# A two-layer mixer block in split fp32: the FFN and short-conv products take the high weights times both halves of x in one 512-column matmul

## The chip, the cores and the metric

The kernel runs on one core of one Trainium2 chip. The metric is the device time of one execution in microseconds (us), the median of the runs shown. "TensorE", "VectorE" and "ScalarE" are the core's engines; SBUF is its working memory, PSUM (eight banks of 512 fp32 columns on 128 partitions) is where TensorE writes.

## The reference

256 tokens of width 1024 go through two layers of one kind and a third of another. A layer is FFN, mixer, FFN, each with a norm before and after it; the mixer is a short convolution in the first layer and a gated delta rule in the second. Then come a second mixer (sparse attention and RWKV side by side) and an FFN with a convolution. All of it is fp32.

```python
def swiglu(x, w_gate_up, w_down):
    gate, up = jnp.split(x @ w_gate_up, 2, axis=-1)      # 1024 -> 2 x 2816
    return (jax.nn.silu(gate) * up) @ w_down              # 2816 -> 1024

def short_conv_mixer(x, w_in, conv_w, w_out):
    b, c, v = jnp.split(x @ w_in, 3, axis=-1)             # 1024 -> 3 x 1024
    y = b * causal_depthwise_conv(c * v, conv_w)
    return y @ w_out                                      # 1024 -> 1024

for i in range(DEPTH):                                    # two layers
    ff = swiglu(rms_norm(h, g[0]), ffn_w_gate_up[i, 0], ffn_w_down[i, 0])
    h = h + 0.5 * rms_norm(ff, g[1])
    m_in = rms_norm(h, g[2])
    mix = short_conv_mixer(m_in, ...) if i % 2 == 0 else gated_deltanet_mixer(m_in, ...)
    h = h + rms_norm(mix, g[3])
    ff = swiglu(rms_norm(h, g[4]), ffn_w_gate_up[i, 1], ffn_w_down[i, 1])
    h = h + 0.5 * rms_norm(ff, g[5])
# then the second mixer with its output projection, and an FFN whose hidden width is
# 2 x 2816, convolved over three tokens, gated and projected down to 1024
```

## The kernel before, in words

Activations lie transposed: 128 features on the partitions, 256 tokens along the row. A product is a list of 128 x 128 weight tiles (`Product`, L47): column tiles (128 output features each) times row tiles (128 input features). The first column tiles are taken as a group, row tile by row tile; `groups` names the sizes, and the rest go one by one. There are 968 chunks of four weight tiles, 3872 tiles in all, in the order of `SEQUENCE` (L111).

Every product runs in three matmuls per weight tile, in fp32r (a form of fp32 that TensorE streams in one pass). Weights and operand are each split in a high part and the low rest, and the product is wh xh + wh xl + wl xh (`mm3`, L790). Each matmul has its own load of 128 x 128 weights (the row PEld), also where two in a row use the same weights. Row tiles 0 and 1 of a group of six use another order (`mm3s`, L797).

The weights come by DMA from the SP queue into six raw buffers (`Streamer`, L620); for each chunk ScalarE copies the high half (`whi<-wraw`) and VectorE subtracts for the low one (`wlo<-wraw,whi`), into a ring of seven chunks.

The operand x is h times a gain, split the same way by `split_x` (L815) in `prepare` (L821), without the factor 1/rms of the norm, which is not known yet. `stat_now` (L959) makes 1/rms (`rb`) after the first group with a product with a matrix of ones, in plain fp32, and the evacuation multiplies by it. In the delta rule's input product, the second mixer's `rw` product and the convolution FFN (`cup`), all grouped 6, 2, 2, x is split again with 1/rms in it (`again`, `resplit`, L1050) for the column tiles after these ten.

What is evacuated: an up product's pair of column tiles (gate, up) gets two VectorE products with `rb`, SiLU on ScalarE, a product, a high copy and a low subtract (`swiglu`, L987). Short conv's triples (L1012) and the convolution FFN's pairs (L2108) go through a few VectorE steps per tap. A down product's column goes through `post` (L965): a square, its sum, and the product with its gain. PSUM: with the banks taken in turn, column tiles that are taken one by one share a bank by twos where the evacuation takes pairs or triples; in a group, and in the down products, each has a bank (`dense_steps`, L903).

The order on each engine is written by a planner (`Pace`, L260). It prices each instruction (a matmul: columns / 2400 us + 2.5 ns), builds the graph of what waits for what, tries some list schedules (`ranks`, L335; `schedule`, L363), and `arrange` (L446) fixes the best order. The delta rule and the second mixer weave their own small products between those of the weight stream.

Of the kernel before, what the change touches and what calls it, by code (L numbers as in the profile page):

```python
# [12 lines left out]
F32R = mybir.dt.float32r  # L13
# [61 lines left out]
# The rule's input projection by column tile: queries 0-7, keys 8-15, values 16-31, output gates 32-47, and 48 for beta  # L75
# and the decay. The keys come first, whose inverse takes longest.
# [3 lines left out]
def products():  # L80
    g = {}
    for l in range(2):
        for j in range(2):
            g["up", l, j] = Product("ffn_w_gate_up", (l, j), KD, _blocks(_pairs(0, FF, NF)), [6])
            g["down", l, j] = Product("ffn_w_down", (l, j), NF, _blocks(range(0, D, P)))
# [3 lines left out]
    g["sc_in"] = Product("sc_w_in", (0,), KD, _blocks(c), [6])  # L89
# [148 lines left out]
class Staged:  # L238
    """Work on a sequence of items, whose later stages are issued with the next items' earlier ones."""
# [20 lines left out]
class Pace:  # L260
    """An account, by rough prices in us, of when each engine gets to what is issued to it and when each part of a
    tile was last written and read. Independent sequences of steps are interleaved by it."""
# [17 lines left out]
    def parts(self, ap):  # L280
        """The pieces of its tile that an access pattern touches."""
# [18 lines left out]
    def when(self, *aps):  # L300
        """When everything issued to these is done."""
# [144 lines left out]
    def arrange(self, tc, rank):  # L446
        """Has each engine take what was issued to it in the order of these ranks."""
# [8 lines left out]
    def node(self, engine, op, out, ins, outs, price):  # L456
        """An instruction of the graph, with those that come before it."""
# [132 lines left out]
class Chain:  # L590
    """A sequence of steps with the banks and buffers that it takes in turn."""
# [15 lines left out]
def alternate(*steps):  # L607
    """The sequences in turn, each waiting while another goes on."""
# [11 lines left out]
class Streamer:  # L620
    """Brings the weight tiles on chip ahead of their use, as high and low halves."""
# [43 lines left out]
    def split_to(self, c):  # L665
        """Every chunk before this one."""
# [3 lines left out]
    def split_ahead(self, c):  # L670
        """While chunk c is in use and as long as the engines that split have little else to do."""
# [22 lines left out]
class Kernel:  # L694
    def __init__(self, nc, pool, psum, wstream, params, consts, xt, lowrank, w1, out):
# [9 lines left out]
        self.xh = pool.tile([P, KD, T], F32R, name="xh")  # L705
        self.xl = pool.tile([P, KD, T], F32R, name="xl")
# [14 lines left out]
        self.x0 = [pool.tile([P, T], F32R, name=f"x0{i}") for i in range(2)]  # L721
# [21 lines left out]
    def warm(self):  # L743
        """Products of nothing in use, by which the tensor engine's clock is up when the first operands are there."""
# [8 lines left out]
    def region(self, tag, dtype=F32):  # L753
        """A region of SBUF for a phase's tiles: a new tile in the place of the last one."""
# [3 lines left out]
    def hidden(self, **kept):  # L758
        """Room for both parts of a branch's hidden tiles."""
        a = [kept.get(t) or self.region(t, F32R) for t in ("a0", "a1", "a2")]  # L760
        slot = lambda n: a[n // 16][:, n % 16 * T:(n % 16 + 1) * T]
        self.hid = [(slot(k), slot(NF + k)) for k in range(NF)]
# [16 lines left out]
    def bank(self, n=7):  # L779
        """The next of the first n banks, or of a list of banks."""  # L780
# [9 lines left out]
    def mm3(self, out, xh, xl, start, stop):  # L790
        wh, wl = self.W.next()
        nc = self.nc
        nc.tensor.matmul(out, wh, xh, start=start, stop=False)
        nc.tensor.matmul(out, wh, xl, start=False, stop=False)
        nc.tensor.matmul(out, wl, xh, start=False, stop=stop)

    def mm3s(self, outs, xs, start):  # L797
        """A row tile of a group, the products with the operand's low part last; the first tile's operand may be a sum."""
        mm = self.nc.tensor.matmul
        ws = [self.W.next() for _ in outs]  # L800
        for n, (xh, xl) in enumerate(xs):
# [13 lines left out]
    def split_x(self, k, gain):  # L815
        """The product of h tile k with a gain, split for the tensor engine."""
# [4 lines left out]
    def prepare(self, k, gain, post=None):  # L821
        """h tile k takes its update, and its product with the next gain is split for the tensor engine. Of the first
        tile only the update's is split, which is added to that of h before it."""
        nc = self.nc
        h = self.h[:, k, :]
        if post is not None:
            t = self.temp()
            if k == 0:
                self.first = gain
                nc.pace.hurry = URGENT  # L830
                nc.vector.tensor_mul(self.x0[0], self.fg0, post)
                nc.pace.hurry = 0.0
                nc.vector.tensor_mul(t, self.fg0, post)
                nc.vector.tensor_sub(self.x0[1], t, self.x0[0])
# [16 lines left out]
    def halves(self, out, w, x, **kw):  # L851
        """A product with few columns, on each half of the tensor engine's."""
# [4 lines left out]
    def take(self, *aps):  # L857
        """The next bank of the running sequence, once it and these are ready."""
# [44 lines left out]
    def dense_steps(self, key, x, evac, step, prepare=None, hooks=(), each=None, at_group=None, late=None, banks=7, lead=LEAD, gate=None):  # L903
        """One product: evac gets the PSUM regions of `step` consecutive column tiles; hooks[g] runs when the
# [1313 lines left out]
```

## Time and profile before

| | |
|---|---|
| three runs | 1584.44, 1581.71, 1584.09 us; median 1584.09 us |
| the profiled execution | span 1586.4 us, first to last instruction (the page gives no other time of its own) |
| TensorE matmul / weight load rows busy | 99% / 96%, 13544 each |
| VectorE / ScalarE busy | 76% / 65% |
| DMA | 261 MB, 165 GB/s in the mean |

The profile shows one execution. Where instructions of one engine overlap, busy time counts the overlap once, while the mean of one is its full length; the pace of an engine is read from starts, or from a stretch's length over its count. Matmul ends are modelled. All operations carry one line (L576, the helper that issues them), so groups are told apart by their tiles: `xh`, `xl` and `x` are the operand's halves and the first tile's (x0), `a` the hidden tiles, `whi` and `wlo` the split weights.

Where the stages lie, in us from the start: up(0,0) to 130, down(0,0) to 194, short conv in 194 to 264 and out to 288, up(0,1) to 415, down(0,1) to 478, up(1,0) to 601, down(1,0) to 665, delta rule to 930, up(1,1) to 1058, down(1,1) to 1121, second mixer to 1374 with its output product to about 1396, convolution FFN up to 1520 and down to the end.

### The profile page before, as it was taken

To read this page: it belongs to the slowest core of one execution; us is meant where nothing else is said; L and a number is where in the kernel's file an instruction comes from. 1 tells how busy PE (TensorE), PEld (TensorE's weight loads), DVE (VectorE), ACT (ScalarE), POOL (GpSimd) and SP (SyncE) were. 2 spreads that over 40 slices of the span, in tenths; PEclk is the share of its full clock that TensorE was granted. 3 is DMA by queue.
4 is the path that set the end of the run, shared out by engine and by line. 5 is a ranking of instruction groups with operands and counts; after the bars stand their busy time and mean duration, and the time that the engine had idled before them with its cause. 6 is when DMAs were issued, how large, how long until landed. Compare 5 with 4: busy or idle time off the path is not lost.

```text
span 1586.4 us, 35927 instructions
## 1 busy us (share of the span) xinstructions
PE 1569.7 (99%) x13544; PEld 1517.6 (96%) x13544; DVE 1202.2 (76%) x2527; ACT 1026.9 (65%) x2153; POOL 10.4 (1%) x24
## 2 busy tenths in 40 slices
PE   9999999999999999999999999999999999999999
PEld 9999999999999999989898999999987877999999
DVE  7776597877658777689996778765887955889973
ACT  7555566765557557578887866555782766578763
POOL 0000000000000000000000000000010000000000
PEclk9999999999999999999999999999998989999999
DMA  8666556566665667525342456666533312566664
GB/s 275 192 186 187 180 176 186 170 190 187 184 185 167 201 193 245 180 79 168 116 138 81 135 159 201 187 187 184 168 106 101 120 35 87 172 187 188 187 194 118
DMA packets 142670, 261.14 MB, mean 165 GB/s; under 512 B 15904, under 2 KB 17952, under 8 KB 142368
## 3 DMA queue, kind: packets, MB, share of 16 engines
q1 hardware_dynamic: 142496, 258.84, 53.9%
q8 instruction: 106, 1.74, 0.4%
q14 instruction: 68, 0.56, 0.1%
HBM read 257.73 MB, written 1.05 MB: 163 GB/s over the span
## 4 chain that ended last, share of the span: by engine, by line
PE 93%; DVE 3%; ACT 2%; issue 1%; DMA 0%; SPq 0%; DVEq 0%
PE bank L576 93%; DVE a L576 1%; ACT a L576 1%; DVE wlo L576 1%; ACT stm L576 1%; DMA wraw<-wstream 0%; DVE arG L576 0%; ACT whi L576 0%; DVE stm L576 0%; ACT arG L576 0%; DVE fg L576 0%; DVE xl L576 0%; DVE tmp L576 0%; DVE acc L576 0%; ACT pad L576 0%
## 5 line engine op out<-in xcount | busy, mean ns | idle before, releaser
L576 ACT ACTIVATE whi<-wraw 128x512 fp32r<-128x512 f32 x956 | 599.3, 630 | 440.9 <-PE bank L576 335.5
L576 DVE TENSOR_TENSOR wlo<-wraw,whi 128x512 fp32r<-128x512 f32 x956 | 653.0, 688 | 291.2 <-ACT whi L576 282.6
L576 PE MATMUL bank<-xh,whi 128*128 128x256 f32 x2688 | 753.1, 284 | 6.1 <-DVE stm L576 3.6
L576 PE MATMUL bank<-xh,wlo 128*128 128x256 f32 x2688 | 751.6, 284 | 0.0
L576 PE MATMUL bank<-xl,whi 128*128 128x256 f32 x2688 | 745.7, 282 | 0.7 <-DVE xl L576 0.7
L576 PEld LDWEIGHTS bank<-xh,whi 128*128 128x128 f32 x2688 | 507.6, 190 | 15.2 <-issue 6.0
L576 PEld LDWEIGHTS bank<-xl,whi 128*128 128x128 f32 x2688 | 504.1, 189 | 8.8 <-issue 6.6
L576 PEld LDWEIGHTS bank<-xh,wlo 128*128 128x128 f32 x2688 | 502.0, 189 | 6.9 <-issue 6.0
L576 PE MATMUL bank<-a,whi 128*128 128x256 f32 x2272 | 411.0, 283 | 0.2
L576 PEld LDWEIGHTS bank<-a,whi 128*128 128x128 f32 x2272 | 353.6, 191 | 1.2 <-DVE a L576 0.4
L576 PE MATMUL bank<-a,wlo 128*128 128x256 f32 x1136 | 321.6, 283 | 0.0
L576 PEld LDWEIGHTS bank<-a,wlo 128*128 128x128 f32 x1136 | 217.2, 191 | 0.0
L576 DVE TENSOR_TENSOR tmp<-bank,rb 128x256 f32<-128x256 f32 x176 | 66.3, 418 | 8.0 <-ACT rb L576 0.6
L576 PE MATMUL bank<-a 64*128 64x256 f32 (+3 forms) x192 | 41.4, 397 | 1.4 <-DVE arG L576 1.4
L576 ACT ACTIVATE xh<-h,par 128x256 fp32r<-128x256 f32 x70 | 34.0, 498 | 12.0 <-DVE h L576 9.9
L576 ACT ACTIVATE arG<-bank 128x256 f32<-128x256 f32 (+2 forms) x87 | 37.8, 443 | 5.2 <-PE bank L576 4.9
L576 DVE SCALAR_TENSOR_TENSOR arG<-arG,par 128x256 f32<-128x256 f32 x88 | 40.0, 477 | 0.0
L576 ACT ACTIVATE a<-tmp 128x256 fp32r<-128x256 f32 x88 | 35.7, 406 | 6.5 <-DVE tmp L576 6.3
L576 DVE TENSOR_TENSOR acc<-acc,tmp 128x256 f32<-128x256 f32 x92 | 38.4, 418 | 2.0 <-ACT acc L576 0.9
L576 DVE TENSOR_TENSOR a<-tmp,a 128x256 fp32r<-128x256 f32 x88 | 36.7, 417 | 3.8 <-ACT a L576 3.8
L576 ACT ACTIVATE tmp<-tmp 128x256 f32<-128x256 f32 x88 | 35.4, 407 | 3.8 <-DVE tmp L576 3.7
L576 DVE TENSOR_TENSOR tmp<-tmp,tmp 128x256 f32<-128x256 f32 x88 | 36.7, 417 | 0.0
(253 smaller groups left out, 1229.5 us busy)
## 6 DMA issues: line engine op xcount, KB each, us to landing
wraw<-wstream SPq DMA_DIRECT2D x968, 256.0 KB, 2.8
arG<-cmp_w SPq DMA_DIRECT2D x1, 1024.0 KB, 4.7
out_dram<-h SPq DMA_DIRECT2D x8, 128.0 KB, 2.7
con<-consts SPq DMA_DIRECT2D x1, 734.0 KB, 4.7
h<-xt SPq DMA_DIRECT2D x1, 512.0 KB, 6.5
a<-lowrank SPq DMA_DIRECT2D x1, 512.0 KB, 4.0
par<-params SPq DMA_DIRECT2D x1, 283.5 KB, 4.8
h<-xt SPq DMA_DIRECT2D x2, 128.0 KB, 3.4
```

Of the source, the lines that this page charges most:

```text
L576: i = f(*args, **kw)
```

## The change

x, the first tile's update x0 and the hidden tiles put each tile's high and low half side by side, so that the two are 512 columns in one row. A column tile for which `wide` holds takes a whole bank: one matmul of the high weights with both halves, 512 columns, and one of the low weights with the high half into the bank's first 256. The two halves of the bank are added when it is evacuated, by a ScalarE copy and a VectorE add. Wide are: in the four up products and cup the column tiles after the first 10 (of 44), in sc_in after the first 9 (of 24), and all but the last of the eight in the down products, sc_out, out2 and cdown. The up products take groups of 6, 2, 2, sc_in of 6, 3, and x is split again with 1/rms in it before the wide tiles of these five; their evacuation no longer multiplies by `rb`. The gate and up tiles move from the general buffers to eight slots in the region arG. Descriptions in the code are removed as well, which changes nothing.

```diff
-            g["up", l, j] = Product("ffn_w_gate_up", (l, j), KD, _blocks(_pairs(0, FF, NF)), [6])
+            g["up", l, j] = Product("ffn_w_gate_up", (l, j), KD, _blocks(_pairs(0, FF, NF)), [6, 2, 2])
...
-    g["sc_in"] = Product("sc_w_in", (0,), KD, _blocks(c), [6])
+    g["sc_in"] = Product("sc_w_in", (0,), KD, _blocks(c), [6, 3])
...
+        self.x = pool.tile([P, KD, 2, T], F32R, name="x")
+        self.xh, self.xl = self.x[:, :, 0], self.x[:, :, 1]
...
+        self.hid = [a[k // 8][:, k % 8 * 2 * T:(k % 8 + 1) * 2 * T].rearrange("p (w t) -> p w t", w=2) for k in range(NF)]
...
+    def mm2(self, out, x, start, stop):
+        wh, wl = self.W.next()
+        nc = self.nc
+        nc.tensor.matmul(out, wh, x.rearrange("p w t -> p (w t)"), start=start, stop=False)
+        nc.tensor.matmul(out[:, :T], wl, x[:, 0], start=False, stop=stop)
+
+    def onto(self, m, r):
+        h = self.h[:, m, :]
+        if r.shape[1] == 2 * T:
+            t = self.temp()
+            self.nc.scalar.activation(t, r[:, T:], AF.Copy)
+            self.nc.vector.tensor_add(h, h, t)
+            r = r[:, :T]
+        self.nc.vector.tensor_add(h, h, r)
+
+    def total(self, out, r):
+        self.nc.scalar.activation(out, r[:, T:], AF.Copy)
+        self.nc.vector.tensor_add(out, r[:, :T], out)
...
             for i in range(n):
-                half = (c + i) % step % 2 if n == 1 else 0
+                both = wide is not None and wide(c + i)
+                half = (c + i) % step % 2 if n == 1 and not both else 0
                 if not half:
                     b = self.bank(banks(g) if callable(banks) else banks)
                     yield self.when(b)
-                rs.append(b[:, half * T:(half + 1) * T])
+                rs.append(b if both else b[:, half * T:(half + 1) * T])
...
-                        self.mm3(r, *x(c + i, k), k == 0, k == p.kt - 1)
+                        (self.mm3 if r.shape[1] == T else self.mm2)(r, x(c + i, k), k == 0, k == p.kt - 1)
...
     def post(self, m, r, gain, then):
+        if r.shape[1] == 2 * T:
+            t = self.temp()
+            self.total(t, r)
+            r = t
...
+        G = self.region("arG")
         def s0(i, r, c):
-            c["g"], c["u"] = self.temp(), self.temp()
-            nc.vector.tensor_mul(c["g"], r[0], self.rb)
-            nc.vector.tensor_mul(c["u"], r[1], self.rb)
+            c["g"], c["u"] = (G[:, (2 * i + n) % 8 * T:((2 * i + n) % 8 + 1) * T] for n in range(2))
+            for t, b in zip((c["g"], c["u"]), r):
+                if i < 5:
+                    nc.vector.tensor_mul(t, b, self.rb)
+                else:
+                    self.total(t, b)
...
+        again = self.again(pre_gain)
+        self.dense(("up", l, j), self.x, evac, 2, prepare, [lambda: self.stat_now(self.rb)],
+                   each=lambda k: k < 4 or again(k - 4), at_group=2, late=again, wide=lambda c: c >= 10)
...
+        self.dense(("down", l, j), self.hx, lambda m, r: self.post(m, r[0], post_gain, then), 1, wide=lambda c: c < KD - 1)
...
-            nc.vector.tensor_mul(t, c, rsq)
-            nc.vector.tensor_mul(d["b"], b, self.rb)
+            if i < 3:
+                nc.vector.tensor_mul(t, c, rsq)
+                nc.vector.tensor_mul(d["b"], b, self.rb)
+            else:
+                self.total(t, c)
+                u = self.temp()
+                self.total(u, v)
+                self.total(d["b"], b)
+                v = u
...
+        self.dense("sc_in", self.x, evac, 3, prepare, [first],
+                   each=lambda k: k < 4 or again(k - 4), at_group=1, late=again, wide=lambda c: c >= 9)
...
             for u in range(2):
+                s = d["s"][u][:, 2:]
                 if i < 5:
-                    nc.vector.tensor_mul(d["s"][u][:, 2:], r[u], self.rb)
-                    src = d["s"][u][:, 2:]
+                    nc.vector.tensor_mul(s, r[u], self.rb)
                 else:
-                    nc.scalar.activation(d["s"][u][:, 2:], r[u], AF.Copy)
-                    src = r[u]
-                nc.scalar.activation(d["y"][u], src, AF.Identity, scale=w(2, i + NF * u))
+                    self.total(s, r[u])
+                nc.scalar.activation(d["y"][u], s, AF.Identity, scale=w(2, i + NF * u))
```

## Rows read from the trace of the kernel before

**Rows 1.** The page, span and part 1: busy us (share) xinstructions.
```profile
span 1586.4 us, 35927 instructions
PE 1569.7 (99%) x13544; PEld 1517.6 (96%) x13544; DVE 1202.2 (76%) x2527; ACT 1026.9 (65%) x2153; POOL 10.4 (1%) x24
```
**Rows 2.** The page, part 4: the chain that ended last, by engine.
```profile
PE 93%; DVE 3%; ACT 2%; issue 1%; DMA 0%; SPq 0%; DVEq 0%
```
**Rows 3.** The page, part 5: busy us, mean ns of one, idle before.
```profile
L576 PE MATMUL bank<-xh,whi 128*128 128x256 f32 x2688 | 753.1, 284 | 6.1 <-DVE stm L576 3.6
```
**Rows 4.** Windows by stage: busy us (xcount) of PE, PEld, DVE, ACT, POOL; clock, DMA.
```profile
131.00:193.00 62.00, 62.00 (x519) 62.00 (x518) 32.73 (x53) 33.95 (x62) 0.00 (x0) 1.00 0.62 185
...
212.00:264.00 52.00, 52.00 (x444) 51.95 (x443) 46.40 (x97) 30.30 (x55) 0.00 (x0) 1.00 0.66 199
265.00:287.00 22.00, 22.00 (x186) 22.00 (x185) 13.60 (x26) 14.74 (x32) 0.00 (x0) 1.00 0.62 185
...
305.00:414.00 109.00, 109.00 (x927) 108.95 (x927) 83.45 (x170) 64.83 (x124) 0.00 (x0) 1.00 0.64 193
...
502.00:601.00 99.00, 99.00 (x874) 98.92 (x874) 78.20 (x159) 61.47 (x120) 0.00 (x0) 1.00 0.67 198
...
1410.00:1519.00 109.00, 109.00 (x927) 109.00 (x927) 105.06 (x224) 88.71 (x203) 0.00 (x0) 1.00 0.64 186
1520.00:1582.00 62.00, 62.00 (x519) 62.00 (x519) 32.55 (x56) 25.95 (x45) 0.00 (x0) 1.00 0.55 159
```
**Rows 5.** Timeline in up(0,0): start us, us, engine, operation.
```profile
60.00 0.28 PE L576 MATMUL bank<-xh,wlo 128*128 128x256 f32 x1
60.00 0.19 PEld L576 LDWEIGHTS bank<-xh,whi 128*128 128x128 f32 x1
60.11 0.28 PE L576 MATMUL bank<-xh,whi 128*128 128x256 f32 x1
60.12 0.19 PEld L576 LDWEIGHTS bank<-xl,whi 128*128 128x128 f32 x1
```
**Rows 6.** Timeline in the delta rule: four products of 16 columns.
```profile
690.62 0.53 PEld L576 LDWEIGHTS bank<-arM,con 128*128 128x128 f32 x4
690.73 0.51 PE L576 MATMUL bank<-arM,con 128*128 128x16 f32 x4
```
**Rows 7.** The product with ones: the timeline, and 25 to 26.2 us by lines.
```profile
25.65 0.59 PE L576 MATMUL bank<-acc,con 128*128 128x256 f32 x2
...
L576 PE MATMUL bank<-acc,con 128*128 128x256 f32 x2 | 0.6, 378 | 0.0
```
**Rows 8.** At the halved clock: the window, and two starts of the timeline.
```profile
1283.80:1285.20 1.40, 1.40 (x7) 1.40 (x7) 0.00 (x0) 0.26 (x1) 0.00 (x0) 0.50 0.00 0
...
1284.29 0.41 PE L576 MATMUL bank<-xh,whi 128*128 128x256 f32 x1
...
1284.50 0.41 PE L576 MATMUL bank<-xl,whi 128*128 128x256 f32 x1
```
**Rows 9.** Timeline of VectorE in the convolution FFN's up product.
```profile
1470.99 0.69 DVE L576 TENSOR_TENSOR wlo<-wraw,whi 128x512 fp32r<-128x512 f32 x1
1471.60 0.48 DVE L576 SCALAR_TENSOR_TENSOR arG<-arG,par 128x256 f32<-128x256 f32 x1
1471.99 0.42 DVE L576 TENSOR_TENSOR a<-arG,a 128x256 fp32r<-128x256 f32 x1
1472.33 0.48 DVE L576 SCALAR_TENSOR_TENSOR arG<-arG,par 128x256 f32<-128x256 f32 x1
```
**Rows 10.** Windows where x is split again, or would be.
```profile
197.00:212.00 15.00, 15.00 (x134) 15.00 (x133) 14.64 (x37) 11.82 (x27) 0.00 (x0) 1.00 0.37 115
...
508.00:518.00 10.00, 10.00 (x90) 10.00 (x90) 10.00 (x24) 7.40 (x17) 0.00 (x0) 1.00 0.68 207
...
1408.00:1423.00 15.00, 15.00 (x128) 14.95 (x127) 13.52 (x30) 11.59 (x24) 0.00 (x0) 1.00 0.62 182
```

More of the change, by code (lines that the diff above doesn't have):

```diff
@@ L720, in __init__ @@
         self.fg0 = self.pad[4][:, 3:]
-        self.x0 = [pool.tile([P, T], F32R, name=f"x0{i}") for i in range(2)]
+        self.x0 = pool.tile([P, 2, T], F32R, name="x0")
         self.first = None
@@ L800, in mm3s @@
         ws = [self.W.next() for _ in outs]
-        for n, (xh, xl) in enumerate(xs):
+        for n, x in enumerate(xs):
+            xh, xl = x[:, 0], x[:, 1]
             for r, (wh, _) in zip(outs, ws):
@@ L901, in weave, with dense_steps @@
                 c.ready = y or 0.0
-    def dense_steps(self, key, x, evac, step, prepare=None, hooks=(), each=None, at_group=None, late=None, banks=7, lead=LEAD, gate=None):
+    def dense_steps(self, key, x, evac, step, prepare=None, hooks=(), each=None, at_group=None, late=None, banks=7, lead=LEAD, gate=None, wide=None):
         p = PRODUCTS[key]
         if not callable(x):
-            x = lambda c, k, hl=x: (hl[0][:, k, :], hl[1][:, k, :])
+            x = lambda c, k, both=x: both[:, k]
         regions = []
@@ L928, in dense_steps @@
                         late(i)
-                if k < 2 and n == 6:
+                if k < 2 and n == 6 and rs[0].shape[1] == T:
                     xs = [x(c, k)]
@@ L1039, in s3 @@
             nc.vector.tensor_mul(d["y"], d["y"], d["b"])
-            nc.scalar.activation(self.hid[i][0], d["y"], AF.Copy)
+            nc.scalar.activation(self.hid[i][:, 0], d["y"], AF.Copy)
         def s4(i, r, d):
-            nc.vector.tensor_sub(self.hid[i][1], d["y"], self.hid[i][0])
+            nc.vector.tensor_sub(self.hid[i][:, 1], d["y"], self.hid[i][:, 0])
         self.hidden()
         evac = Staged(s0, tap(1), tap(0), s3, s4)
-        self.dense("sc_in", (self.xh, self.xl), evac, 3, prepare, [first])
-        self.dense("sc_out", self.hx, lambda m, r: self.post(m, r[0], post_gain, then), 1)
+        again = self.again(pre_gain)
+        self.dense("sc_in", self.x, evac, 3, prepare, [first],
+                   each=lambda k: k < 4 or again(k - 4), at_group=1, late=again, wide=lambda c: c >= 9)
+        self.dense("sc_out", self.hx, lambda m, r: self.post(m, r[0], post_gain, then), 1, wide=lambda c: c < KD - 1)
     def resplit(self, k, gain):
@@ L1362, in chain @@
             r0, r1 = self.region("a0", F32R), self.region("a1", F32R)
-            oh, ol = (r.rearrange("p (h t) -> p h t", t=T) for r in (r1, r0))
+            both = [r.rearrange("p (h w t) -> p h w t", w=2, t=T) for r in (r0, r1)]
+            o = lambda n: both[n // 8][:, n % 8]
             kept.update(a0=r0, a1=r1)
@@ L1438, in side @@
             yield from chain()
[L1440 removed]
+        x = self.x
         def out_ready(g, k):
@@ L1802, in gnorm @@
             r = self.region("a0", F32R)
-            h, l = split["rwkv"] = t256(r[:, 0:1024]), t256(r[:, 1024:2048])
-            split["nsa"] = t256(r[:, 2048:3072]), t256(r[:, 3072:4096])
+            both = r.rearrange("p (n k w t) -> p n k w t", n=2, w=2, t=T)
+            split["rwkv"], split["nsa"] = both[:, 0], both[:, 1]
+            h, l = both[:, 0, :, 0], both[:, 0, :, 1]
             lw = lambda n: par(n)[:, :, None].to_broadcast([P, 4, P])
@@ L2050, in attention @@
             yield lambda: "nsa" in split
-            h, l = split["nsa"]
+            h, l = split["nsa"][:, :, 0], split["nsa"][:, :, 1]
             for i in range(4):
@@ L2084, in proj_ready @@
                 yield until(name)
-                yield self.when(*split["rwkv" if g else "nsa"])
+                yield self.when(split["rwkv" if g else "nsa"])
         def add(m, r):
-            nc.vector.tensor_add(self.h[:, m, :], self.h[:, m, :], r[0])
+            self.onto(m, r[0])
         def main():
@@ L2095, in main @@
             yield from self.dense_steps("merge", x, merge_evac, 2, banks=2)
-            yield from self.dense_steps("proj", lambda c, k: tuple(a[:, k] for a in split["rwkv" if c >= KD else "nsa"]),
+            yield from self.dense_steps("proj", lambda c, k: split["rwkv" if c >= KD else "nsa"][:, k],
                                         Staged(p0, p1, p2), 1, banks=2, gate=proj_ready)
             self.bank_at = 2
-            yield from self.dense_steps("out2", x, add, 1, banks=7)
+            yield from self.dense_steps("out2", x, add, 1, banks=7, wide=lambda c: c < KD - 1)
         again = self.again(gain)
@@ L2140, in s3 @@
             nc.vector.tensor_mul(d["y"][0], d["y"][0], d["y"][1])
-            nc.scalar.activation(self.hid[i][0], d["y"][0], AF.Copy)
+            nc.scalar.activation(self.hid[i][:, 0], d["y"][0], AF.Copy)
         def s4(i, r, d):
-            nc.vector.tensor_sub(self.hid[i][1], d["y"][0], self.hid[i][0])
+            nc.vector.tensor_sub(self.hid[i][:, 1], d["y"][0], self.hid[i][:, 0])
         again = self.again(gain)
-        self.dense("cup", (self.xh, self.xl), Staged(s0, tap(1), tap(0), s3, s4), 2,
+        self.dense("cup", self.x, Staged(s0, tap(1), tap(0), s3, s4), 2,
                    lambda k: self.prepare(k, gain), [lambda: self.stat_now(self.rb)],
-                   each=lambda k: k < 4 or again(k - 4), at_group=2, late=again)
+                   each=lambda k: k < 4 or again(k - 4), at_group=2, late=again, wide=lambda c: c >= 10)
         def add(m, r):
-            nc.vector.tensor_add(self.h[:, m, :], self.h[:, m, :], r[0])
+            self.onto(m, r[0])
             nc.sync.dma_start(self.out[m * P:(m + 1) * P, :], self.h[:, m, :])
-        self.dense("cdown", self.hx, add, 1)
+        self.dense("cdown", self.hx, add, 1, wide=lambda c: c < KD - 1)
     def run(self):
```

49 lines of the change are left out of this document (22 added, 27 removed).

## The prediction

> **What bounds the kernel now.** I read the engine summary first, then the chain of waits, the stretches by stage, and last single instructions in the timeline. The summary has TensorE's matmul row busy for 99% of the span, VectorE for 76%, ScalarE for 65% [rows 1], and the chain that ended last is 93% matmul [rows 2]. That is not yet a verdict, as a matmul is shown for 284 ns while the next starts much earlier [rows 3]. The stretches by stage give the real pace: length over matmul count. It is 62 us / 519 = 119.5 ns in a down product, 109 / 927 = 117.6 ns in an up product and in the convolution FFN's, 99 / 874 = 113.3 ns in up(1,0), 117.1 ns in the short conv's input, 118.3 ns in its output [rows 4]; up(0,0) and up(1,1) go as up(0,1), the other three down products of the FFNs as the first. The granted clock is 1.00 (2.4 GHz) in all of them. 256 columns, one per cycle, would be 106.7 ns. So each matmul loses 7 to 13 ns, and there are no gaps between them: it is lost inside a steady rhythm.
>
> The timeline shows the rhythm [rows 5]: the load for the next matmul starts as the present matmul starts and never earlier, so a period is at least one load. How long is a load by itself? Four products of 16 columns answer it: almost nothing streams, yet their loads start (0.53 - 0.19) / 3 = 0.113 us apart [rows 6]. And a long stream with a load behind it: the plain fp32 product with the ones matrix is two records, whose starts are 0.59 - 0.378 = 0.21 us apart [rows 7], which is 512 columns at the full clock (213 ns) with nothing lost. I read this so: at 256 columns the load (113 ns) is longer than the stream (107 ns) and sets the period; at 512 the load disappears.
>
> **The change part by part.**
>
> *TensorE.* For a wide tile the matmuls go from 3 x 256 columns to 512 + 256; one load of the high weights goes. Wide are 34 of 44 column tiles times 8 row tiles in each of four up products (272 each), 7 x 22 = 154 in each down product, 15 x 8 = 120 in sc_in, 56 in sc_out, 56 in out2, 272 in cup, 154 in cdown: 2362 of 3872 tiles. The projections of the delta rule and of the second mixer stay as they are. The trace has no 512-column fp32r matmul. From below, a new tile is 213 + 107 = 320 ns (streams alone); from above it is the present tile (340 to 358 ns), if the stream itself is slow. I take 215 ns, by the ones product as the nearest row, plus 120 ns for the short one, whose successor's load is as exposed as now: 335 ns. Savings:
> - three up products at 352.8 ns: 816 x 17.8 ns = 14.5 us
> - up(1,0) at 339.8: 272 x 4.8 = 1.3 us
> - four down products at 358.4: 616 x 23.4 = 14.4 us
> - sc_in 120 x 16.4 = 2.0 us, sc_out 56 x 19.8 = 1.1 us
> - out2, for which I took no row and use the fastest stage: 0.3 us
> - cup 272 x 17.8 = 4.8 us, cdown 154 x 23.4 = 3.6 us
>
> Sum 42.0 us on the engine that sets the end.
>
> *Evacuation.* A wide tile adds one ScalarE copy and one VectorE add; in the up products the add takes the place of the product with 1/rms, in sc_in two adds take the place of two products and a third is new, in cup both adds per pair are new. VectorE's prices, start to start in a full queue: 0.61 us for a 512-column subtract, 0.39 us for a scalar_tensor_tensor, 0.34 us for a 256-column add or product [rows 9]. A pair of cup (16 tiles, 4 weight chunks) needs 4 x 0.61 + 4 x 0.39 + 2 x 0.34 = 4.7 us now, within 16 x 352.8 ns = 5.64 us; yet VectorE's row is already busy 105 of 109 us [rows 4], as dependent steps wait for each other. Two adds more make 5.4 us against a new TensorE time of 16 x 335 ns = 5.36 us. VectorE becomes the bound there: I take cup's pace to stay at 5.64 us a pair and strike its 4.8 us. At worst it runs at 6.0 us and loses 17 pairs x 0.36 = 6 us more. An up pair needs 4 x 0.61 + 4 x 0.34 = 3.8 us, which fits. ScalarE at 89 of 109 us in cup [rows 4] swaps its scaled reads of PSUM for reads of SBUF and stays below its limit; elsewhere it is at 60% and has room for two short copies per pair.
>
> *The second split of x.* Each up product and sc_in now split x again with 1/rms in it: 8 x (0.34 + 0.39) = 5.9 us of VectorE within about 14 us, the groups after the first. These stretches are full already: VectorE is busy 14.6 of 15 us at the start of the short conv, 46.4 of 52 us through the rest of it, 10 of 10 us early in up(1,0) [rows 4, 10]. The cover is the split weights waiting ahead in a ring of seven chunks. Cup does the same now, with more VectorE work per pair, and its matmul row shows 15.0 of 15 us there [rows 10], so for the up products I take only 0.5 us of stall each (2.0 us; 0 to 2 us each). In sc_in VectorE needs 36 chunks x 0.61 + 8 triples x (6 x 0.34 + 2 x 0.39) + 5.9 = 50 us for some 49 us of TensorE: I strike its 2.0 us and add 2.0 us of stall (0 to 6 us).
>
> *Hidden at no cost.* The extra sum in post, and the extra add of out2 and cdown, stand beside the next column's 7 us of matmuls, with VectorE at half load [rows 4]; the last column stays narrow, so the tail is as now. A 512-column matmul also needs the low half of its operand at once: the last hidden tile is used 21 tiles (7 us) into the down product, later than its subtract. Whole banks leave seven tiles in flight (7 x 8 x 335 ns = 19 us) against an evacuation of some 3 us. The gate tiles' new place in arG has to be free before the delta rule's weights are put there early; those come behind chunks already queued. The weight stream runs 5% faster at a DMA share of 0.64 [rows 4]: room enough.
>
> 42.0 - 4.8 - 2.0 - 2.0 - 2.0 = 31 us. The profiled span of 1586.4 us [rows 1] becomes 1555 us; it is 2.3 us over the median of the runs, so 1584.1 becomes 1553 us.
>
> **The rivals.**
>
> (A) The stream, not the load, takes the 113 to 119.5 ns, in proportion to its columns. Then 512 columns cost twice that, and each tile saves only what is fixed per matmul, about 2 ns by the ones product: 2362 x 2 ns = 4.7 us. The vector work then decides the sign: about 1.5 us of stall in each up product and 4 us in sc_in, 10 us together, give 1584 - 5 + 10 = 1589 us, slower. For it: at the halved clock a matmul takes 0.21 us, that is 213 ns and nothing lost [rows 8], as if an operand read too fast were what costs at the full clock. Against it: the 16-column products have the 113 ns without any stream, and the ones product streams 512 cycles without loss (though as plain fp32, which reads half as fast). It decides as soon as a new tile exceeds some 349 ns. The Trainium skill, page "TensorE: Matmul & The Clock Gate", section "Back-to-back issue gap", comes to a like time by another way: a matmul at the full clock takes its columns / 2.4 plus 2.5 ns. By that rule a tile goes from 327 to 325 ns and the change is worth about 6 us of matmul; this trace has 113 to 119.5 ns where the rule has 109, and that excess is what the forecast rests on.
>
> (B) VectorE takes back more: cup at 6.0 us a pair, 2 us in each up product, 6 us in sc_in. 31 - 6 - 6 - 4 = 15 us saved, 1569 us. For it: the full stretches [rows 10]. Against it: at a full row VectorE still has waits in it that a deeper queue closes.
>
> (C) The exposed load falls back to 113 ns after each long matmul and cup follows TensorE: 328 ns a tile is 16.5 us more, with cup 21 us: 1532 us.
>
> **How the numbers follow.** Forecast 0.62, (B) 0.18, (C) 0.07, (A) 0.13. Around the forecast alone, with tiles from 328 to 343 ns and the stalls' bounds: 1535 to 1572 us. The order of work in the delta rule and the second mixer is planned anew by the same prices, which can shift either by some us. The range takes in (B) and the better part of (C) and leaves (A) out: 1530 to 1578 us. A measurement of this kernel can't tell less than 0.2% (3.2 us) from nothing. (A) splits into slower 0.08 and no difference 0.05; (B) with stalls twice as long adds 0.02 to slower and 0.01 to no difference: faster 0.84, the same 0.06, slower 0.10.
>
> **What would show it.** Down products: 22 tiles of a column in 7.4 us where they take 7.9 us; a long matmul about 215 ns before the next start and a short one 113 to 120 ns. A long one at 226 to 240 ns is (A). Cup: pairs at 5.6 us with VectorE full and matmuls waiting for banks or split weights; 5.36 us would show VectorE's cost overrated, 6.0 us is (B). In sc_in and at the start of the up products: idle TensorE released by VectorE. The forecast is wrong if the down products, which have no vector trouble, don't gain some 3.5 us each.

## The result, and the profile after

The changed kernel takes 1594.8 us (median of 8 runs, 1591.1 to 1603.4) where the kernel before takes 1582.9 us beside it: a ratio of 1.0075, interval [1.0052, 1.0099]. It is slower by 12 us; the forecast was 31 us faster, the range ended at 1578 us. On TensorE it is rival (A) that happened.

The page after: the span, the first three engines, the chain by engine, and three groups of part 5 (busy us, mean ns of one, idle before).

```profile
span 1592.3 us, 31702 instructions
...
PE 1568.7 (99%) x11182; PEld 1405.9 (88%) x11182; DVE 1254.9 (79%) x2695; ACT 1106.6 (69%) x2393; POOL 10.4 (1%) x24
...
PE 91%; DVE 4%; ACT 2%; DMA 1%; issue 1%; SPq 0%; DVEq 0%; ACTq 0%
...
L576 PE MATMUL bank<-x,whi 128*128 128x256 f32 (+1 forms) x3900 | 973.8, 330 | 7.5 <-DVE stm L576 3.6
...
L576 PE MATMUL bank<-a,whi 128*128 128x512 f32 (+1 forms) x1446 | 407.4, 351 | 0.7 <-DVE a L576 0.5
L576 PE MATMUL bank<-a,wlo 128*128 128x256 f32 x1136 | 321.0, 283 | 6.1 <-DVE wlo L576 6.1
```

TensorE issues 2362 matmuls and as many loads fewer than in [rows 1], which is the number of wide tiles, and its row is busy for the same time. The last group shows the one new thing on it: 6.1 us of waits for low halves of weights.

What a wide tile takes is in the timeline of up(0,0), at the place of [rows 5] (start us, us, engine, operation):

```profile
60.03 0.40 PE L576 MATMUL bank<-x,whi 128*128 128x512 f32 x1
...
60.26 0.28 PE L576 MATMUL bank<-x,wlo 128*128 128x256 f32 x1
...
60.38 0.40 PE L576 MATMUL bank<-x,whi 128*128 128x512 f32 x1
```

From start to start: 0.23 us after the long one, 0.12 us after the short one. At the trace's full resolution they are 235 and 118 ns, 353 ns a tile, where three matmuls took 353 ns as well. In the down products it is 237 and 117 ns in the mean, 353.4 ns a tile, against 360.0 ns. By stage (windows; busy us with the number of instructions of PE, PEld, DVE, ACT and POOL, then granted clock, DMA share, GB/s):

```profile
131.00:193.00 62.00, 62.00 (x372) 54.76 (x371) 35.52 (x60) 37.31 (x70) 0.00 (x0) 1.00 0.64 187
212.00:264.00 52.00, 52.00 (x326) 46.54 (x325) 50.25 (x111) 35.38 (x75) 0.00 (x0) 1.00 0.67 207
...
305.00:414.00 109.00, 109.00 (x657) 96.44 (x656) 88.92 (x184) 77.62 (x165) 0.00 (x0) 1.00 0.65 196
502.00:605.00 103.00, 103.00 (x604) 90.30 (x603) 82.66 (x172) 72.78 (x157) 0.00 (x0) 1.00 0.64 191
```

The matmul row is full and the clock is whole in all of them, as in [rows 4]; there are fewer matmuls and each is longer. Stage by stage, from the first matmul of a product to the first of the next, the profiled executions differ so: each down product 62.6 us against 63.6 (four: -4.0), short conv's output -0.6, its input +0.2, up(0,0), up(0,1) and up(1,1) +0.1, +0.8 and +0.2, up(1,0) 127.1 against 123.2 (+3.9), out2 with cup +0.9, and cdown 75.5 against 66.7 (+8.8). Before the first product 0.8 is added. The delta rule's input is +2.4; the second mixer -7.6 (the mean granted clock there is 0.94 in the kernel before's profile and 0.98 in this one, with 27 and 10 us at the halved clock). The sum is +5.9 us, the difference of the spans; the medians are 6 us further apart, since the profiled execution of the kernel before lies some 5 us above its median (a run's time is 2 us longer than its span) and that of the changed kernel does not.

So the place that costs most is the passage from cup to cdown. Windows there (the first line is from cup):

```profile
1440.00:1460.00 20.00, 20.00 (x115) 17.39 (x114) 18.88 (x42) 15.70 (x35) 0.00 (x0) 1.00 0.61 179
...
1510.00:1515.00 5.00, 5.00 (x31) 4.35 (x30) 4.50 (x12) 3.70 (x10) 0.00 (x0) 1.00 0.33 100
1515.00:1520.00 5.00, 4.70 (x27) 3.86 (x26) 4.66 (x13) 3.91 (x12) 0.00 (x0) 1.00 0.19 63
1520.00:1525.00 5.00, 3.06 (x16) 2.17 (x15) 4.99 (x13) 4.44 (x11) 0.00 (x0) 1.00 0.31 104
1525.00:1530.00 5.00, 1.10 (x6) 0.73 (x4) 5.00 (x14) 2.63 (x7) 0.00 (x0) 0.78 0.18 52
1530.00:1535.00 5.00, 4.51 (x15) 3.50 (x15) 5.00 (x13) 1.88 (x5) 0.00 (x0) 0.54 0.44 119
```

Up to 1515 us cup's matmul row is full: a wide tile starts every 353.3 ns, so a pair of 16 tiles takes 5.65 us. Then TensorE stands for 6.1 of 15 us while VectorE is full and the weight stream dries up, and after these waits the granted clock falls to 0.54, that is mostly 1.2 GHz. What VectorE does in that time, by groups (xcount, busy us, mean ns), from 1515 to 1532 us of after:

```profile
L576 DVE SCALAR_TENSOR_TENSOR arG<-arG,par 128x256 f32<-128x256 f32 x19 | 8.4, 477 | 0.0
L576 DVE TENSOR_TENSOR wlo<-wraw,whi 128x512 fp32r<-128x512 f32 x6 | 4.1, 683 | 0.0
```

and from 1515 to 1530 us of the kernel before:

```profile
L576 DVE TENSOR_TENSOR wlo<-wraw,whi 128x512 fp32r<-128x512 f32 x11 | 7.4, 689 | 0.9 <-ACT whi L576 0.8
L576 DVE SCALAR_TENSOR_TENSOR arG<-arG,par 128x256 f32<-128x256 f32 x8 | 3.4, 477 | 0.0
```

The SCALAR_TENSOR_TENSOR group is the convolution, four such steps a pair. When cup's last matmul starts, at 1516.6 us of after and 1519.6 us of before, 18 and 6 of them are still to come: four and a half pairs against one and a half. Cdown's weights queue for their split among them, and each late one is a stall (timeline of after, TensorE's waits in brackets):

```profile
1518.87 0.39 PE L576 MATMUL bank<-a,wlo 128*128 128x256 f32 x1 [0.30 <-DVE wlo L576]
...
1521.59 0.39 PE L576 MATMUL bank<-a,wlo 128*128 128x256 f32 x1 [1.07 <-DVE wlo L576]
...
1524.14 0.39 PE L576 MATMUL bank<-a,wlo 128*128 128x256 f32 x1 [0.87 <-DVE wlo L576]
...
1529.70 0.58 PE L576 MATMUL bank<-a,wlo 128*128 128x256 f32 x1 [3.90 <-DVE wlo L576]
...
1530.77 0.80 PE L576 MATMUL bank<-a,whi 128*128 128x512 f32 x1 [0.48 <-DVE a L576]
```

With the matmuls at the halved clock, cdown's starts are some 9.8 us late in sum; the kernel before has none there.

### The profile page after: what moved, and what is told of

It reads as the page before. It is cut to its first block, busy times and chain, and to the rows that moved or that the text cites. A ratio compares the mean times of both kernels' runs of the same rounds, so it can differ in the third digit from the quotient of the medians.

```text
span 1592.3 us, 31702 instructions
## 1 busy us (share of the span) xinstructions
PE 1568.7 (99%) x11182; PEld 1405.9 (88%) x11182; DVE 1254.9 (79%) x2695; ACT 1106.6 (69%) x2393; POOL 10.4 (1%) x24
## 4 chain that ended last, share of the span: by engine, by line
PE 91%; DVE 4%; ACT 2%; DMA 1%; issue 1%; SPq 0%; DVEq 0%; ACTq 0%
PE bank L576 91%; DMA wraw<-wstream 1%; DVE arG L576 1%; DVE a L576 1%; DVE wlo L576 1%; ACT whi L576 1%; ACT a L576 1%; ACT arG L576 0%; DVE stm L576 0%; ACT stm L576 0%; DVE fg L576 0%; SPq L576 0%; DVE x L576 0%; ACT tmp L576 0%; DVE acc L576 0%
## 5 line engine op out<-in xcount | busy, mean ns | idle before, releaser
L576 PE MATMUL bank<-x,whi 128*128 128x256 f32 (+1 forms) x3900 | 973.8, 330 | 7.5 <-DVE stm L576 3.6
L576 PE MATMUL bank<-x,wlo 128*128 128x256 f32 x2718 | 757.6, 284 | 0.0
L576 PEld LDWEIGHTS bank<-x,whi 128*128 128x128 f32 x3900 | 649.7, 189 | 95.1 <-issue 11.8
L576 PEld LDWEIGHTS bank<-x,wlo 128*128 128x128 f32 x2718 | 506.1, 189 | 7.2 <-issue 6.0
L576 PE MATMUL bank<-a,whi 128*128 128x512 f32 (+1 forms) x1446 | 407.4, 351 | 0.7 <-DVE a L576 0.5
L576 PEld LDWEIGHTS bank<-a,whi 128*128 128x128 f32 x1446 | 252.6, 190 | 41.0 <-DVE a L576 1.4
L576 ACT ACTIVATE arG<-bank 128x256 f32<-128x256 f32 (+2 forms) x228 | 89.2, 395 | 5.3 <-PE bank L576 4.7
L576 DVE TENSOR_TENSOR arG<-bank,arG 128x256 f32<-128x256 f32 x175 | 72.6, 418 | 7.7 <-ACT arG L576 7.5
L576 ACT ACTIVATE arG<-arG 128x256 f32<-128x256 f32 (+1 forms) x146 | 65.7, 454 | 3.3 <-DVE arG L576 3.0
L576 ACT ACTIVATE a<-arG 128x256 fp32r<-128x256 f32 (+1 forms) x122 | 50.7, 420 | 11.0 <-DVE arG L576 4.3
```

The lines of the kernel that those rows point to most:

```text
L576: i = f(*args, **kw)
```

## The experiments

Three theories were told apart. **S**, the stream: a matmul with four-byte operands takes a time in proportion to its columns, some 0.45 ns each, and nothing is won by joining two. **L**, the load: the loads are exposed, and something in the new order keeps them so. **V**, VectorE: what was lost beyond that comes from cup's two added sums per pair. Two weaker rivals were the operands' addresses (S1) and the sequence of the three matmuls (R1); against them stood S2 and R2, a rhythm that some disturbance sets.

**Addresses.** The kernel before with all later buffers 32 bytes on:

```diff
+        self.shift = pool.tile([P, 8], F32, name="shift")
```

> The kernel before, with everything behind the first parameter buffer moved by 32 bytes in SBUF, so that x, the hidden tiles and the split weights start at a multiple of 64 bytes where they start 32 beyond one now; the work is the same. Theory S1 (the operand's stream is slowed by where its rows lie in SBUF): matmuls of 256 columns go to about 109 ns or change by several ns in every stage, that is 40 to 100 us off the time, or as much on it. Theory S2 (the stream's pace is a rhythm that the matmuls fall into and that a disturbance sets, whatever the addresses): 113, 118 and 120 ns stay, in much the same stages, and the time stays within 5 us of the kernel before.

1586.6 us, ratio 1.0009 [0.9987, 1.0031]. The down products take 63.6 us as before, and the up products 127 to 128 us: only up(1,0) left its faster pace (126.9 us against 123.2). That the operands begin 32 bytes beyond a multiple of 64 is not what costs, and S1 falls.

**Cup narrow.** The changed kernel with cup's product, and cup's alone, in three matmuls:

```diff
+        if r.shape[1] == T:
+            self.nc.scalar.activation(out, r, AF.Copy)
+            return
...
-                   each=lambda k: k < 4 or again(k - 4), at_group=2, late=again, wide=lambda c: c >= 10)
+                   each=lambda k: k < 4 or again(k - 4), at_group=2, late=again)
```

The first lines stand in `total`: a narrow result is copied by ScalarE, without an add.

> The changed kernel with the convolution FFN's up product narrow again (three matmuls of 256 columns, pairs in one bank, no added VectorE adds); everything else as changed. Theory V (the loss is VectorE's: two adds more per pair there leave it behind, and TensorE waits at the start of the last down product): the gap of some 9 us before the last down product goes, the time falls by 8 to 12 us, to that of the kernel before. Theory T (the loss lies in the matmuls of all stages): it falls by at most 2 us.

1580.8 us, ratio 0.9987 [0.9973, 1.0000]: 14 us below the changed kernel. At the end of cup and the start of cdown (windows, columns as above):

```profile
1505.00:1510.00 5.00, 5.00 (x46) 5.00 (x45) 4.89 (x11) 4.04 (x11) 0.00 (x0) 1.00 0.73 201
1510.00:1515.00 5.00, 5.00 (x40) 4.75 (x39) 4.65 (x12) 4.55 (x12) 0.00 (x0) 1.00 0.66 180
1515.00:1520.00 5.00, 5.00 (x30) 4.39 (x29) 4.92 (x12) 3.73 (x9) 0.00 (x0) 1.00 0.44 136
1520.00:1525.00 5.00, 4.87 (x28) 3.98 (x27) 3.63 (x8) 2.66 (x5) 0.00 (x0) 1.00 0.84 246
```

No hole: 4.87 of 5 us at the least, and the clock stays whole. Cdown's stage is 65.9 us (66.7 in the kernel before), out2 with cup 143.3 (146.1). V is shown as the cause of the hole: the added sums gone, VectorE has the time and TensorE no longer waits for low halves. With it gone the rest of the change is worth nothing that can be told from zero, as S has it; of the 3 us between the medians, the 2.8 us of cup come of a faster pace of its narrow matmuls (114 ns in place of 118), which nothing in the edit asks for. Whether another order of VectorE's queue, cdown's splits ahead of the convolution, would have closed the hole too was not tried.

**Only the down products wide.** No second split, no added sum per pair: the changed kernel with `wide` taken from all up products, from sc_in and cup (out2 keeps it, which the expectation did not say).

```diff
-            g["up", l, j] = Product("ffn_w_gate_up", (l, j), KD, _blocks(_pairs(0, FF, NF)), [6, 2, 2])
+            g["up", l, j] = Product("ffn_w_gate_up", (l, j), KD, _blocks(_pairs(0, FF, NF)), [6])
...
-        self.dense(("up", l, j), self.x, evac, 2, prepare, [lambda: self.stat_now(self.rb)],
-                   each=lambda k: k < 4 or again(k - 4), at_group=2, late=again, wide=lambda c: c >= 10)
+        self.dense(("up", l, j), self.x, evac, 2, prepare, [lambda: self.stat_now(self.rb)])
```

Sc_in and cup lose theirs in the same way, and the up products and sc_in multiply by `rb` at the evacuation again.

> Wide tiles in the six down products and the short conv's output alone; the up products, the short conv's input, the output product of the second mixer and the convolution FFN's up product are as in the kernel before (no second split of x, groups of six). By the trace of the changed kernel a wide down product is 1.0 us shorter (62.6 us for 63.6), so with five of them and sc_out this kernel should be 5 to 6 us faster than the one before. If instead wide tiles gain nothing and the 1.0 us is chance, the time is within 2 us of the kernel before.

1570.5 us, ratio 0.9926 [0.9901, 0.9951]: faster than both kernels, by 12 to 13.5 us (the ratio and the medians) and by 24 us. A down column's timeline:

```profile
139.69 0.39 PE L576 MATMUL bank<-a,whi 128*128 128x512 f32 x1
139.92 0.28 PE L576 MATMUL bank<-a,wlo 128*128 128x256 f32 x1
140.04 0.39 PE L576 MATMUL bank<-a,whi 128*128 128x512 f32 x1
140.27 0.28 PE L576 MATMUL bank<-a,wlo 128*128 128x256 f32 x1
140.38 0.39 PE L576 MATMUL bank<-a,whi 128*128 128x512 f32 x1
```

The long one takes 230 ns, not 237, the tile 347 ns, the down product 61.5 us. That is 2.05 us less in each of the four, 8.2 us of the profile's gain; sc_out and cdown, which are wide too, take 1.0 and 0.8 us less. So some 10 us lie in the wide products, and nearly half of that hangs on the pace of 230 ns, which the changed kernel's down products do not have. The rest is not tied to the edit: sc_in and out2 with cup take 1.6 and 2.8 us less with their narrow matmuls at 114 in place of 118 ns, up(1,0) gives 3.7 back, and the second mixer's 10.8 us, the largest part of the profile's difference, has no wide tile in it: 217 us is its time in the shifted kernel too, and 227.5 that of the one profile of before, whose granted clock there is 0.94 where both others have 0.99.

**384 columns.** The changed kernel, in which the long matmul of the inner row tiles leaves out the last 128 columns (there, half of the tokens miss the product of the high weights with the low half of x):

```diff
+        n = 512 if start or stop else 384
-        nc.tensor.matmul(out, wh, x.rearrange("p w t -> p (w t)"), start=start, stop=False)
+        nc.tensor.matmul(out[:, :n], wh, x.rearrange("p w t -> p (w t)")[:, :n], start=start, stop=False)
```

> The changed kernel with the long matmul cut to 384 columns in all but the first and the last row tile of a wide column tile; it leaves out the product of the high weights with the low part of the last 128 tokens there. Theory S (the stream takes the time, in proportion to its columns): 384 columns take 3/4 of 235 ns, 176 ns (down products 174 to 181). Rival L (a cost per matmul or per load on top of 107, 160 and 213 ns): 166 to 172 ns with the excess of 256 columns (6 to 13 ns), or 182 with that of 512 (22 ns). The short ones stay at 118 ns by both.

1498.3 us, one run, 96 us less than the changed kernel. In up(0,0) (timeline):

```profile
79.84 0.34 PE L576 MATMUL bank<-x,whi 128*128 128x384 f32 x1
80.02 0.28 PE L576 MATMUL bank<-x,wlo 128*128 128x256 f32 x1
80.14 0.34 PE L576 MATMUL bank<-x,whi 128*128 128x384 f32 x1
...
80.74 0.40 PE L576 MATMUL bank<-x,whi 128*128 128x512 f32 x1
80.98 0.28 PE L576 MATMUL bank<-x,wlo 128*128 128x256 f32 x1
```

0.18 us for 384 columns beside 0.24 for 512 and 0.12 for 256. Over all of them 176 to 179, 232 to 234 and 118 ns: 0.45 to 0.47 ns a column at each size, where one column per cycle of the full clock would be 0.417. It is the stream that is slow, and a fixed part that could be saved is at most a few ns.

**The kernel before in bf16.** The split halves are written as bf16 in place of fp32r, so each is rounded more coarsely; two more lines of the edit, not shown, keep the regions' size in bytes.

```diff
-F32R = mybir.dt.float32r
+F32R = mybir.dt.bfloat16
```

> The kernel before with all split operands (weights, x, hidden tiles) kept in bf16 where they were fp32r: the same matmuls, loads, splits and evacuations, half the bytes for TensorE to read; the products are rounded more coarsely. Theory S (what slows the stream is reading a 4-byte operand at the full clock): 256 columns fall from 113 to 120 ns to about 109 ns, as in the plain fp32 products that stream at half the rate; 11,600 matmuls x 4 to 11 ns are 80 to 100 us. Rival P (the writing side in PSUM, or a rhythm of the instructions themselves, whatever the operand's width): 113 to 120 ns stay and only VectorE or ScalarE could gain a little: within 15 us of the kernel before.

1489.8 us, ratio 0.9401 [0.9366, 0.9437].

```profile
60.03 0.27 PE L576 MATMUL bank<-xh,wlo 128*128 128x256 bf16 x1
60.14 0.27 PE L576 MATMUL bank<-xh,whi 128*128 128x256 bf16 x1
60.25 0.27 PE L576 MATMUL bank<-xl,whi 128*128 128x256 bf16 x1
60.36 0.27 PE L576 MATMUL bank<-xh,wlo 128*128 128x256 bf16 x1
```

109 ns from start to start, the same in every stage. Over 11616 matmuls, some 8.3 ns each make the 96 us. The columns written to PSUM and the sequence of instructions are the same, so neither of them set the old pace (rival P). By itself this does not tell S from L, as a bf16 load could be the shorter one too; the next run does.

**The changed kernel in bf16.** The same edit of the changed kernel (same coarser halves).

> The changed kernel with all split operands in bf16. Theory S: a wide tile costs 215 + 109 ns and a narrow one 3 x 109 ns, so 512 columns gain only some 2 ns a tile (5 us) on TensorE, and the added work of VectorE with a faster TensorE makes this one no faster than the narrow bf16 kernel, likely 5 to 15 us slower. Rival P: a wide tile stays at 353 ns and the kernel within 15 us of the changed one.

1499.8 us, ratio 0.9470 [0.9436, 0.9504], 10 us more than the kernel before in bf16.

```profile
60.13 0.27 PE L576 MATMUL bank<-x,wlo 128*128 128x256 bf16 x1
60.24 0.38 PE L576 MATMUL bank<-x,whi 128*128 128x512 bf16 x1
60.46 0.27 PE L576 MATMUL bank<-x,wlo 128*128 128x256 bf16 x1
```

215 ns after the long one, 109 after the short one: twice and once the narrow matmul's time, so even here 512 columns win only 2 to 3 ns. And the long one is 20 ns below its 235 ns in fp32r, a time within which a load of 113 ns has long ended: bf16 makes the stream faster. The hole after cup is there again (cdown 72.6 us against 61.0), which covers the 10 us. The Trainium skill, page "TensorE: Matmul & The Clock Gate", section "Back-to-back issue gap", gives columns / 2.4 plus 2.5 ns for the gap of a single matmul at the full clock, an estimate of 109 and 216 ns here. The bf16 runs agree with it to a nanosecond; the fp32r ones, at 113 to 120 and 230 to 237, do not.

**Sequence.** The kernel before with wh xh, wl xh, wh xl in place of wh xh, wh xl, wl xh:

```diff
-        nc.tensor.matmul(out, wh, xl, start=False, stop=False)
-        nc.tensor.matmul(out, wl, xh, start=False, stop=stop)
+        nc.tensor.matmul(out, wl, xh, start=False, stop=False)
+        nc.tensor.matmul(out, wh, xl, start=False, stop=stop)
```

> The kernel before with the second and the third matmul of a tile swapped, so that the two products with x's high half follow each other (as in the first two row tiles of each group of six, which run at 113 ns). Theory R1 (the pace hangs on the sequence of moving operands): up and down products go to 113 ns, 5 to 7 ns off some 8,000 matmuls, 40 us faster. Theory R2 (the pace is a phase that a disturbance sets and the sequence keeps): the stages keep 118 and 120 ns or change among themselves, and the time stays within 8 us.

1591.8 us, ratio 1.0034 [1.0016, 1.0051]: no gain by the sequence, and R1 falls. Most stages are as before; up(0,0) alone runs at 113 ns to its end (123.5 us against 125.2), up(1,0) no longer does (126.9 against 123.2), and the delta rule's input takes 6.8 us more.

**A short matmul of 128 columns.** The changed kernel, in which the matmul with the low weights leaves out half of the tokens in the inner row tiles:

```diff
+        n = T if start or stop else 128
-        nc.tensor.matmul(out[:, :T], wl, x[:, 0], start=False, stop=stop)
+        nc.tensor.matmul(out[:, :n], wl, x[:, 0, :n], start=False, stop=stop)
```

> The changed kernel with the short matmul (low weights) cut to 128 columns in all but the first and the last row tile of a wide column tile; the product of the low weights with the last 128 tokens is left out there. It shows the load by itself: the next tile's weights are loaded while 128 columns (59 ns by theory S) stream. If a load takes 113 ns, as the 16-column products say, the short one stays at 111 to 118 ns and the time hardly falls; if loads are faster than that, it falls towards 59 ns and the kernel by up to 100 us.

1574.4 us, one run, only 20 us less. Matmuls, and then loads, in up(0,0) (timeline):

```profile
59.55 0.22 PE L576 MATMUL bank<-x,wlo 128*128 128x128 f32 x1
59.61 0.45 PE L576 MATMUL bank<-x,whi 128*128 128x512 f32 x1
59.89 0.22 PE L576 MATMUL bank<-x,wlo 128*128 128x128 f32 x1
59.95 0.44 PE L576 MATMUL bank<-x,whi 128*128 128x512 f32 x1
```

```profile
59.55 0.19 PEld L576 LDWEIGHTS bank<-x,whi 128*128 128x128 f32 x1
59.66 0.19 PEld L576 LDWEIGHTS bank<-x,wlo 128*128 128x128 f32 x1
59.89 0.19 PEld L576 LDWEIGHTS bank<-x,whi 128*128 128x128 f32 x1
```

A tile takes 0.34 us. The columns alone would be 640 x 0.46 = 294 ns. What fits is the load: two loads start 0.11 us apart, and then 0.23 us pass, the long stream. At the trace's full resolution that is 108 + 232 = 340 ns. The short matmul's own row is only 0.06 us ahead of the next; what it does not wait, the long one does (0.28 us to the next start). The missing 128 columns win 13 ns, because there the load sets the pace. So a load does take 108 to 113 ns, here and in the 16-column products [rows 6]; at 256 columns it is no longer than the stream.

**Bf16 with the down products wide**, the third experiment's edit on the bf16 version (same coarser halves):

> The split operands in bf16 (coarser rounding than before), the wide matmul only in the down products of the FFNs, the short conv's and the second mixer's output products and the convolution FFN's down product; all up products, the short conv's input and the convolution FFN's up product as in the kernel before, so no second split and no added VectorE work per pair. To be compared with the kernel before in bf16 (1489.8 us). Stream theory: 2 to 3 ns per wide tile remain to be won, what is fixed per matmul; about 880 wide tiles x 2.5 ns = 2 us less, and no gap at the start of the last down product: 1485 to 1490 us. Load theory: a tile that was 3 x 109 ns goes to 215 + 98 (the load as the records show it) = 313 ns, 14 ns less, 880 x 14 = 12 us: 1478 us. Vector theory in its strong form (any added sum at the evacuation costs time): 1495 us or more.

1485.7 us, ratio 0.9377 [0.9352, 0.9402], the fastest kernel of the study, though its interval overlaps that of the bf16 kernel without it. Its down products take 57.7 us against 58.1: 0.4 us for 154 tiles, 2.5 ns a tile. That is the fixed part of a matmul, and S's number; the 14 ns of L are not there. Cdown gains nothing (62.2 us against 61.0), as TensorE waits 1.3 us in it for hidden tiles.

## Why the prediction was wrong

**The failed step** is "I take 215 ns, by the ones product as the nearest row, plus 120 ns for the short one": 335 ns a tile. It measured 353 ns, 235 + 118 in the up products and 237 + 117 in the down products. In the prediction's terms: the 512-column stream was taken to run without loss, and the 7 to 13 ns that a 256-column matmul loses to be the wait for its load; the loss is the stream's own and grows with its columns. The 42.0 us of the sum shrink to what the down products and sc_out show, 4.6 us; up(0,0), up(0,1), up(1,1) and sc_in gained nothing, where 16.5 us stood, and up(1,0) lost 3.9. The 18 ns between 335 and 353 are 20 more in the long matmul and 2 less in the short one. The old tiles were a little off too: a down product's matmul starts every 120.0 ns, where the window count, which takes in a matmul cut by an edge, gave 119.5; that is some 1 us of the 42.

**How the rows misled.** Three rows were put together: a matmul's period (113 to 119.5 ns), a load by itself (113 ns), and a long plain-fp32 stream without loss. The first two are nearly equal, and I took the second for the cause of the first. Equal numbers are no cause: the 16-column products show what a load takes when nothing streams, not that it is what the stream waits for. And the ones product, the only row that seemed to decide, was of another kind of operand, which the text itself noted (it "reads half as fast"). The halved clock with nothing lost [rows 8] was of this very operand, and I weighed it as the weaker, but by itself it could not decide: at 213 ns the stream is longer than a load of 113 ns, so both theories have nothing lost there, unless the load's time doubles as well. The row that did speak against was in the sum itself: a down product's matmuls start every 120 ns, 7 ns more than the load takes, so a load of 113 ns alone could not be what set that period [rows 4].

The experiments decide it: at 384 and 512 columns (the fourth experiment), where the load has long ended, the loss per column is that of 256, and with half the bytes at the full clock it is gone (109 and 215 ns). With the halved clock, this fits a stream that four-byte operands slow at the full clock. Whether the moving operand or the weights do it was not separated by a run. That the loss grows with the columns (11 ns at 256, 16 to 19 at 384, 19 to 23 at 512) while the load behind each matmul is the same points to the moving operand.

**Rival (A)** was right in its mechanism and its decision point ("as soon as a new tile exceeds some 349 ns"), and its 1589 us is 6 us short. The chance of 0.13 was too low. That its time came so near is partly luck, as its vector part was misplaced: it had 1.5 us of stall per up product and 4 us in sc_in, and the measured loss lies at the start of cdown.

**The second split** costs next to nothing: late starts of TensorE are 0.8 us in sc_in in both kernels, and in the up products between 0.7 and 1.7 us against 0.8 to 1.3. Of my 0.5 us in each up product only up(0,0) shows any (0.4 us), and the 2.0 us in sc_in did not come. That the ring of split weights covered it, and had more time as TensorE was slower than forecast, is likely but not shown.

**Cup** went at 5.65 us a pair, as forecast (5.64), though for another reason: TensorE's tile had not become shorter, and VectorE did not hold it back there. (B) had the right place but not the form: the work that did not fit, 17 pairs x 2 adds x 0.34 = 11.6 us, was not paid in the pairs. It was put off, as four and a half pairs of backlog, and paid at the end as some 9.8 us of late starts, the halved clock's among them. I had costed the pace of the stage and not what stands in the queue when it ends. Cdown, counted at -3.6 us, became +8.8.

**Hidden at no cost**: post's extra sum and the adds of out2 and the down products were hidden, and the tail is as before; the down products' matmul row is full (62.00 of 62 us).

## What to carry to other kernels

- Before joining matmuls to save a load, find what sets their pace, from rows of the same operand type at two column counts, one of them so long that a load ends well within it: two durations that happen to agree (113 ns load, 113 to 120 ns stream) don't tell which of them it is.
- An engine at 95% of a stage is priced at the end of the stage: work that does not fit shows as backlog in the next one, where it holds up whatever shares its queue (here the weight splits), not in the pace of its own.
- Widening saves little here even where its evacuation is free: nothing in the up products, at best 2 us in each down product, and cup's two adds per pair lost more than all of it. Half as many operand bytes won some seven times as much as the best widened kernel, at the price of the rounding.

## What was not expected of the hardware

The fp32r stream has several paces at the same clock. For 256 columns 113, 118 and 120 ns occur and for 512 columns 230 and 235 ns, and one of them holds for hundreds of matmuls; in the down products of after 233, 241 and 236 ns take turns, as steadily. In up(1,0) of the kernel before, two matmuls that take 160 and 221 ns to the next start, at 503 us, are followed by 113 ns to the end of the stage, where 118 ns went just ahead; without them, in the shifted and the changed kernel, that product takes 126.9 and 127.1 us against 123.2. The down products of after run at 237 in the mean, those of the third experiment at 230 ns, with the same instructions there and other ones ahead. In bf16 the pace is 109 ns everywhere. What chooses the pace was not found: neither the addresses nor the sequence of the three matmuls explains it, and it moves a stage by up to 4 us, more than most terms of the sum.
